# Two‑layer encoder in split float32: the token halves of the feed forward become the even and the odd tiles, block sums are made per pair of tiles, and the first products run in two column parts

## The chip, the cores and the metric

The kernel runs on one core of one Trainium2 chip. The metric is the device time of one execution in microseconds (us), as the median of several runs. Nothing else of the chip is used: no second core, no host arithmetic.

## What is computed

The reference is an encoder of two layers on 1024 tokens of width 1024 (float32). Each layer is

```
h = rmsnorm(x);  z = h @ w_in                       # 1024 -> Fourier 256, q 512, k 128, v 128, memory q 256
y = concat(fourier_mix, windowed attention (8 query heads, 2 kv heads, window 128, sink), attention to 256 memory rows)
x = x + rmsnorm(rmsnorm_per_group(y) @ w_out)
h = rmsnorm(x);  gate, up = split(h @ w_ffn_in)     # 1024 -> 2 x 2816
x = x + rmsnorm((silu(gate) * up) @ w_ffn_out)      # 2816 -> 1024
```

The order of the tokens matters in the mixing (window of 128, Fourier transform over the sequence). In the feed forward each token stands for itself.

## The kernel before

**Precision.** Every float32 operand is split in two (`split`, L149 to L152): ScalarE casts a high part (L151), VectorE or GpSimd subtracts it from the source and keeps the low part (L152). One product is three matmuls: high x high, high x low, low x high.

**Tiles.** The 1024 tokens are 8 tiles of 128. A tile's normalized rows are transposed on TensorE (L301 `hTp` in `norm_T` for the mixing, L1013 `hTp` in `Blocks.tile` for the feed forward).

**The feed forward's products** are made with seven block products in place of eight (a 2x2x2 scheme with sums). The activations are four blocks: `raw[half, kg]`, where `half` is a half of the tokens (four tiles, 512 columns) and `kg` a half of the 1024 channels. Before the change half 0 is tiles 0 to 3 and half 1 tiles 4 to 7. `Blocks.sum(i, c)` (L1016) makes the right operand of product i for column c, that is 128 of the 512 columns: products 2, 5, 7, 3 take a block as it is (and only split it), products 1, 4, 6 need a sum or difference first (L1031; `Blocks.last`, L1043 and L1044, then turns the raw blocks into what products 7 and 3 need). Products 2 and 4 need half 0 alone; 5, 1, 6, 7, 3 need half 1 too. The left operands are made by `Quad.weights` (a sum of two weight blocks on VectorE, L1074, then a split). One product is 12 matmuls of 512 columns (L1084). `Quad.step` puts the products together: PSUM tiles `qy` (products 2, 4), `qz` (5, 3), `qx` (1, 7), `qw` (6); `snap` copies one out (L1089). A layer has 11 pairs of quads, gate `gq` and up `uq`.

**From the attention to the feed forward.** The loop `for i in range(NT + 4)` in the main function does, for each i, one unit of the windowed attention (tile i), the output projection of tile i-2 (`mix.out`, PSUM `mo`, two residual and norm steps L988, L324, L325, L289), `hb.tile` of tile i-4, and from i = 8 on the block sums and the first products of the first pair: `gq.step(2)`, `gq.step(4)`, `uq.step(2)`, `uq.step(4)`.

**ffn_out** (L1212, PSUM `fo`) uses the same seven products over 22 x 128 channels; `abs_` is the ring of buffers for its split operands. The result of a tile is finished by `last_tile`: residual (L322 Square on ScalarE, L324 on VectorE, L325 add on GpSimd or VectorE), norm (L284, L289), store to `x2d`, and at the next tile the transposition `norm_T` into `nhT`. In the last product (i = 6) the four tiles of half 0 are finished one by one; those of half 1 follow after the last matmul. Between them stands `half()`, which is `mix.zf(0)` of the next layer: the first projection (PSUM `zT`, 48 matmuls of 512 columns) of tiles 0 to 3.

**What sets the order.** The program is one text; when it is built, a scheduler fixes the order of each engine's instructions, and the engines meet at semaphores. Memory is an arena of numbered places; `Ring(...)` lists the places that a kind of buffer goes through in turn, and a place that is still read holds up what is to be written there. DMAs start from the sync engine's (SP) queue in its order.

Of the kernel before, what the change touches and what calls it, by code (L numbers as in the profile page):

```python
# [39 lines left out]
SKEW = 1  # L40
N_SM = {"pos": 1}
# [27 lines left out]
def tile_encoder(ctx: ExitStack, tc: tile.TileContext, T, C, out):  # L69
# [60 lines left out]
    qws, sns, silus, acts = Ring(32, 0, 16, 20), Ring(36, 38, 40, 42, 32, 34), run(8, 5, 2), run(18, 7, 2)  # L130
    sums, wsums = run(8, 4, 2), Ring(4, 6)
# [4 lines left out]
    wcs, abs_ = Ring(112, 116, 96, 100, 48, 52, 56, 60), Ring(80)  # L136
# [170 lines left out]
    def residual_out(x, f, g, dst, t):  # L307
# [689 lines left out]
    class Blocks:  # L997


        HB = {2: (64, 72), 4: (80, 88), 5: (16, 24), 1: (0, 8), 6: (32, 40), 7: (None, None), 3: (None, 104)}  # L1000
# [4 lines left out]
        def tile(self, h, t):  # L1005
            half, c = divmod(t, 4)
# [9 lines left out]
        def sum(self, i, c, lo_eng=None):  # L1016
# [31 lines left out]
    class Quad:  # L1048


        def __init__(self, l, c0, hb):
            self.hb, self.c0 = hb, c0
# [38 lines left out]

        def step(self, i):

            if i == 2:
                self.y = ps([512], "qy", "pT")
                self.product(self.y, 2, True)
                self.s2 = self.snap(self.y)
            if i == 4:
                self.product(self.y, 4, False)
# [56 lines left out]
    def ffn_in(l, hb, actd, first):  # L1156

        for p in range(NFF // 2):
# [10 lines left out]
            if p == 0:  # L1169
                qws.ks, wsums.ks = (44, 48, 52, 56), (4, 6, 0, 2)  # L1170
# [263 lines left out]
```

## Time and profile before

| | |
|---|---|
| median of 3 runs | 2161.32 us (2158.72 to 2163.56) |
| profiled execution | 2151.62 us, of it 2149.5 us span from first to last instruction |
| mean granted TensorE clock | 0.969 of full |
| busy: TensorE / VectorE / ScalarE / GpSimd | 2007.0 / 1625.6 / 1070.4 / 846.9 us |
| chain that ended last | TensorE 73%, VectorE 8%, DMA 7%, GpSimd 4%, ScalarE 4%, issue 3% |

Busy time is what an engine's own instructions cover. PE is TensorE, PEld its weight loads, DVE VectorE, ACT ScalarE, POOL GpSimd, SP the sync engine. "Idle before" an instruction is the time in which its engine had nothing to run, and the name behind the arrow is what ended last before it started. The clock 1.00 is 2.4 GHz, 0.50 is 1.2 GHz; a stretch between them was partly at either.

### The profile page before, as it was taken

To read this page: it belongs to the slowest core of one execution; us is meant where nothing else is said; L and a number is where in the kernel's file an instruction comes from. 1 tells how busy PE (TensorE), PEld (TensorE's weight loads), DVE (VectorE), ACT (ScalarE), POOL (GpSimd) and SP (SyncE) were. 2 spreads that over 40 slices of the span, in tenths; PEclk is the share of its full clock that TensorE was granted. 3 is DMA by queue.
4 is the path that set the end of the run, shared out by engine and by line. 5 is a ranking of instruction groups with operands and counts; after the bars stand their busy time and mean duration, and the time that the engine had idled before them with its cause. 6 is when DMAs were issued, how large, how long until landed. Compare 5 with 4: busy or idle time off the path is not lost.

```text
span 2149.5 us, 28257 instructions
## 1 busy us (share of the span) xinstructions
PE 2007.0 (93%) x9402; PEld 1662.2 (77%) x9402; DVE 1625.6 (76%) x2517; ACT 1070.4 (50%) x2273; POOL 846.9 (39%) x854
## 2 busy tenths in 40 slices
PE   7998999699999999999989989986999999999997
PEld 6787787578888887878868768765888888878785
DVE  7569767998877877657866696779988787876774
ACT  6467767544333334444545686674433333345441
POOL 4244436633423334222454344464433343431322
PEclk9998999899999999999999999996999999999998
DMA  6111222412332326878641123133223232378874
GB/s 222 43 50 64 69 89 99 157 64 93 119 102 94 110 92 211 308 222 294 223 147 42 45 69 107 57 125 111 84 93 118 84 128 93 101 240 301 276 267 137
DMA packets 173602, 287.50 MB, mean 134 GB/s; under 512 B 15480, under 2 KB 73360, under 8 KB 173456
## 3 DMA queue, kind: packets, MB, share of 16 engines
q1 hardware_dynamic: 165392, 266.82, 37.7%
q10 hardware_dynamic: 8064, 18.88, 2.3%
q8 instruction: 74, 1.21, 0.2%
q14 instruction: 72, 0.59, 0.1%
HBM read 219.06 MB, written 66.58 MB: 133 GB/s over the span
## 4 chain that ended last, share of the span: by engine, by line
PE 73%; DVE 8%; DMA 7%; POOL 4%; ACT 4%; issue 3%; SPq 0%; POOLq 0%; ACTq 0%; DVEq 0%
PE fo L1212 12%; PE qz L1084 11%; PE qy L1084 11%; PE qx L1084 11%; PE mo L162 6%; PE qw L1084 5%; PE kvp L162 4%; PE qp L162 3%; DVE arena_r L152 3%; DMA arena_f<-actd 2%; PE sc L728 2%; PE av L772 2%; PE pT L765 1%; ACT arena_r L151 1%; DMA arena_f<-in_w_ffn_out 1%
## 5 line engine op out<-in xcount | busy, mean ns | idle before, releaser
L151 ACT CAST arena_r<-arena_f 128x512 fp32r<-128x512 f32 (+1 forms) x780 | 443.7, 591 | 689.6 <-PE qz L1084 117.2
L152 DVE TENSOR_TENSOR arena_r<-arena_f,arena_r 128x512 fp32r<-128x512 f32 (+1 forms) x676 | 539.4, 821 | 178.5 <-ACT arena_r L151 175.0
L1212 PE MATMUL fo<-arena_r 128*128 128x512 f32 x1848 | 430.9, 395 | 15.2 <-ACT arena_r L151 12.3
L1212 PEld LDWEIGHTS fo<-arena_r 128*128 128x128 f32 x1848 | 350.9, 191 | 91.7 <-ACT arena_r L151 14.8
L1084 PE MATMUL qy<-arena_r 128*128 128x512 f32 x1056 | 264.2, 399 | 24.3 <-ACT arena_r L151 16.5
L1084 PEld LDWEIGHTS qy<-arena_r 128*128 128x128 f32 x1056 | 202.8, 193 | 69.1 <-ACT arena_r L151 17.0
L1074 DVE TENSOR_TENSOR arena_f<-arena_f 128x512 f32<-128x512 f32 x220 | 210.0, 958 | 8.2 <-DMA arena_f<-in_w_ffn_in 3.2
L1084 PE MATMUL qz<-arena_r 128*128 128x512 f32 x704 | 196.2, 389 | 0.0
L1104 POOL TENSOR_TENSOR arena_f<-arena_f 128x512 f32<-128x512 f32 x44 | 70.1, 1593 | 305.8 <-ACT arena_f L1089 305.8
L1196 POOL TENSOR_TENSOR arena_f<-arena_f 128x512 f32<-128x512 f32 x50 | 74.0, 1481 | 267.2 <-DVE arena_r L152 134.7
L1084 PEld LDWEIGHTS qz<-arena_r 128*128 128x128 f32 x704 | 132.6, 188 | 27.6
L1136 POOL TENSOR_TENSOR arena_f<-arena_f 128x512 f32<-128x512 f32 x44 | 73.5, 1672 | 165.2 <-DVE arena_f L1116 127.3
L152 POOL TENSOR_TENSOR arena_r<-arena_f,arena_r 128x256 fp32r<-128x256 f32 (+2 forms) x104 | 85.5, 826 | 130.9 <-ACT arena_r L151 121.5
L1084 PE MATMUL qw<-arena_r 128*128 128x512 f32 x528 | 128.0, 390 | 3.0 <-ACT arena_r L151 3.0
L1084 PE MATMUL qx<-arena_r 128*128 128x512 f32 x528 | 127.3, 389 | 0.0
L1084 PE MATMUL qx<-big,arena_r 128*128 128x512 f32 x528 | 126.8, 389 | 0.0
L1084 PEld LDWEIGHTS qw<-arena_r 128*128 128x128 f32 x528 | 99.2, 188 | 23.9 <-ACT arena_r L151 3.2
L1084 PE MATMUL qz<-big,arena_r 128*128 128x512 f32 x352 | 115.7, 389 | 0.0
L1084 PEld LDWEIGHTS qx<-arena_r 128*128 128x128 f32 x528 | 99.1, 188 | 20.6
L1084 PEld LDWEIGHTS qx<-big,arena_r 128*128 128x128 f32 x528 | 99.1, 188 | 20.6
L162 PE MATMUL mo<-arena_r 128*128 128x512 f32 x384 | 104.8, 415 | 4.5 <-DVE arena_f L988 2.3
L162 PE MATMUL mo<-big,arena_r 128*128 128x512 f32 x384 | 102.7, 404 | 0.2 <-ACT arena_f L948 0.2
(218 smaller groups left out, 3592.8 us busy)
## 6 DMA issues: line engine op xcount, KB each, us to landing
arena_f<-in_w_ffn_out SPq DMA_DIRECT2D x264, 256.0 KB, 4.3
arena_f<-in_w_ffn_in SPq DMA_DIRECT2D x88, 512.0 KB, 3.6
actd<-arena_f SPq DMA_DIRECT2D x154, 256.0 KB, 3.8
arena_f<-actd SPq DMA_DIRECT2D x154, 256.0 KB, 4.2
arena_f<-in_w_in SPq DMA_DIRECT2D x40, 256.0 KB, 2.7
arena_f<-in_x SPq DMA_DIRECT2D x16, 512.0 KB, 4.0
arena_f<-in_w_out SPq DMA_DIRECT2D x32, 256.0 KB, 2.8
pmd<-arena_f ACTq DMA_DIRECT2D x32, 256.0 KB, 2.0
```

The lines of the kernel that those rows point to most:

```text
L151: nc.scalar.copy(hi, src)
L152: return (lo_eng or nc.vector).tensor_tensor(out=lo, in0=src, in1=f32(hi), op=ALU.subtract)
L162: mm(self.dst, a, b, start=self.i == 0, stop=self.i == self.n - 1)
L728: mm(pt, lhs, self.kst[g][i][:, k0 * P : k1 * P], start=i == 0, stop=i == 1)
L765: nc.tensor.transpose(pT[:, h, :], es_[h // 2][:, h % 2, j * P : j * P + P], ident)
L772: mm(av, lhs, p_, start=j == 0 and i == 0, stop=j == nk - 1 and i == 1)
L1074: nc.vector.tensor_tensor(out=s, in0=a, in1=b, op=op)
L1084: mm(pt, a, b, start=start and n == 0, stop=n == 11, skip_group_check=not start)
L1104: nc.gpsimd.tensor_tensor(out=self.v, in0=self.v, in1=self.s2, op=ALU.add)
L1136: (G if i in (0, 3) else V).tensor_tensor(out=a[i], in0=c, in1=g[i], op=ALU.mult)
L1196: (nc.vector, nc.gpsimd)[k % 2].tensor_tensor(out=s, in0=x, in1=y, op=op)
L1212: mm(pt, ab[:, 0, x, sl], ab[:, 1, y], start=new and first and j == 0, stop=last and j == 2, skip_group_check=not new)
```

## The change

1. `TILES = (0, 2, 4, 6, 1, 3, 5, 7)`: `Blocks.tile` puts tile t into half t mod 2, column t div 2. Half 0 is now the even tiles, half 1 the odd ones. `ffn_out` finishes the tiles in the order of `TILES`; n is the position in that order. `half()` (the next layer's `zf(0)`, still tiles 0 to 3) stands after the seventh tile in place of the sixth.
2. In the transition loop the sums for products 2 and 4 are made per pair of tiles as soon as an even tile is there (`i >= 4`), during the attention; those for 5, 1, 6 follow from i = 8 on, three columns ahead of the last tile, the fourth after the loop.
3. `product` takes a column slice, and weights are kept (`self.ws`). `ahead(i, sl)` runs product 2 or 4 of the first pair on columns 0 to 383 (three even tiles), and later on columns 384 to 511.
4. Places move: `HB` of products 4, 5 and 1, `qws` for the first weight loads (8, 12, 0, 44), `wcs` (88, 92 for 112, 116), `sums` (one place, then two, before four), `abs_` of ffn_out in layer 0 (nine places before six, and five for the last product) and in layer 1 (the same fifteen in another order).

```diff
@@ Blocks
-        HB = {2: (64, 72), 4: (80, 88), 5: (16, 24), 1: (0, 8), 6: (32, 40), 7: (None, None), 3: (None, 104)}
+        HB = {2: (64, 72), 4: (80, 112), 5: (0, 8), 1: (16, 24), 6: (32, 40), 7: (None, None), 3: (None, 104)}
...
-            half, c = divmod(t, 4)
+            c, half = divmod(t, 2)
@@ Quad
-        def product(self, pt, i, start):
-            w = self.weights(i)
+        def product(self, pt, i, start, sl=slice(0, 512)):
+            if i not in self.ws:
+                self.ws[i] = self.weights(i)
+            w = self.ws[i]
...
+        def ahead(self, i, sl):
+            if i == 2:
+                if sl.start == 0:
+                    self.y = ps([512], "qy", "pT")
+                    self.s2 = sns(512)
+                self.product(self.y, 2, True, sl)
+                nc.scalar.copy(self.s2[:, sl], self.y[:, sl])
+            else:
+                self.product(self.y, 4, False, sl)
@@ ffn_out
                 if i == 6 and k in (0, 2, 4, 6):
-                    t = (0, 2, 4, 6).index(k)
-                    out(t, fb[t][:, 0])
+                    out(k, fb[k // 2][:, 0])
...
         if not late:
-            out(4, fb[0][:, 1])
-            out(5, fb[1][:, 1])
+            out(1, fb[0][:, 1])
+            out(3, fb[1][:, 1])
+            out(5, fb[2][:, 1])
             half()
-            for p in range(2, 4):
-                out(4 + p, fb[p][:, 1])
+            out(7, fb[3][:, 1])
@@ the loop from the attention to the feed forward
+            c, odd = divmod(i - 4, 2)
+            if i >= 4 and not odd:
+                hb.sum(2, c)
+                hb.sum(4, c)
             if i == NT:
-                for c in range(4):
-                    hb.sum(2, c)
+                sums.ks = (40, 42)
+                gq.load()
+                gq.ahead(2, slice(0, 384))
+                for c in range(2):
+                    hb.sum(5, c)
             if i == NT + 1:
-                gq.load()
-                for c in range(4):
-                    hb.sum(4, c)
-                gq.step(2)
+                uq.load()
+                uq.ahead(2, slice(0, 384))
+                gq.ahead(4, slice(0, 384))
+                uq.ahead(4, slice(0, 384))
+                hb.sum(5, 2)
+                for c in range(3):
+                    hb.sum(1, c)
             if i == NT + 2:
-                uq.load()
-                gq.step(4)
-                uq.step(2)
-                uq.step(4)
-            if i >= NT:
-                for n in (5, 1):
-                    hb.sum(n, i - NT)
-            if i > NT:
-                for c in (i - NT - 1,) if i < NT + 3 else (2, 3):
+                for n in (2, 4):
+                    for q in first:
+                        q.ahead(n, slice(384, 512))
+                for c in range(3):
                     hb.sum(6, c)
                     hb.last(c)
+        for n in (5, 1, 6):
+            hb.sum(n, 3)
+        hb.last(3)
@@ ffn_out's ring, layer 1 then layer 0
-        abs_.ks = (64, 72, 80, 88, 16, 24, 0, 8, 32, 40, 48, 56, 96, 104, 112) if last else (80, 88, 48, 56, 96, 104)
+        abs_.ks = (64, 72, 80, 112, 0, 8, 16, 24, 88, 96, 32, 40, 48, 56, 104) if last else (64, 72, 80, 112, 88, 96, 48, 56, 104)
```

The order of instructions shows the moves best. In the rows below the first number is a line of the kernel's own text (after the change the lines of the helpers are two higher, and L1084 is L1082, L1013 is L1015, L1074 is L1070, L289 is L291).

TensorE in layer 0, from the last output projections (`mo` of tile 7 is the pair 4014/4028 before, 4039/4053 after) to the feed forward; `hTp` are the transpositions of the tiles, two per tile, the last two of tile 7. Before:

```order
L162 MATMUL mo_4028<-arena_r 128x512 x12
L1013 MATMUL hTp_4064<-const,arena_f 128x128 x4
L1084 MATMUL qy_4084<-arena_r 128x512 x2
L1013 MATMUL hTp_4111<-const,arena_f 128x128 x4
L1013 MATMUL hTp_4117<-const,arena_f 128x128 x4
L1084 MATMUL qy_4084<-arena_r 128x512 x22
L1084 MATMUL qy_4139<-arena_r 128x512 x2
L1013 MATMUL hTp_4180<-const,arena_f 128x128 x4
L1084 MATMUL qy_4139<-arena_r 128x512 x10
L1013 MATMUL hTp_4186<-const,arena_f 128x128 x4
L1084 MATMUL qw_4263<-arena_r 128x512
L1084 MATMUL qy_4139<-arena_r 128x512 x12
```

After:

```order
L164 MATMUL mo_4053<-arena_r 128x512 x8
L1082 MATMUL qy_4018<-arena_r 128x384 x2
L1015 MATMUL hTp_4083<-const,arena_f 128x128 x4
L1015 MATMUL hTp_4089<-const,arena_f 128x128 x4
L1082 MATMUL qy_4018<-arena_r 128x384 x10
L164 MATMUL mo_4053<-arena_r 128x512 x4
L1082 MATMUL qy_4018<-arena_r 128x384 x12
...
L1082 MATMUL qy_4097<-arena_r 128x128
L1015 MATMUL hTp_4235<-const,arena_f 128x128 x4
L1082 MATMUL qy_4018<-arena_r 128x128 x11
L1082 MATMUL qy_4097<-arena_r 128x128 x11
L1015 MATMUL hTp_4241<-const,arena_f 128x128 x4
```

The first products start before the last output projection is done, and all 48 + 48 of their matmuls stand ahead of the last transposition of tile 7; before, 12 of the 48 stood behind it.

VectorE in layer 0 at the first weight sum of the first pair (L1074 before, L1070 after; L988 and L990 finish `mo`, L289 and L291 are a tile's norm). Before:

```order
L988 SCALAR_TENSOR_TENSOR arena_f<-mo_4028,grs_3939,arena_f 128x512
L152 TENSOR_TENSOR arena_r<-arena_f,arena_r 128x4x128
L289 SCALAR_TENSOR_TENSOR arena_f<-arena_f,nrs_3982 128x1024
L1031 TENSOR_TENSOR arena_f<-big_3470,big_3992 128x512
L1044 TENSOR_TENSOR big_3985<-big_3985,big_3992 128x4x128
L152 TENSOR_TENSOR arena_r<-big_3992,arena_r 128x4x128
L1074 TENSOR_TENSOR arena_f<-arena_f 128x512
```

After:

```order
L990 SCALAR_TENSOR_TENSOR arena_f<-mo_3953,grs_3821,arena_f 128x512
L1070 TENSOR_TENSOR arena_f<-arena_f 128x512
L990 SCALAR_TENSOR_TENSOR arena_f<-mo_3967,grs_3821,arena_f 128x512
L154 TENSOR_TENSOR arena_r<-arena_f,arena_r 128x512
L1070 TENSOR_TENSOR arena_f<-arena_f 128x512
...
L990 SCALAR_TENSOR_TENSOR arena_f<-mo_4053,grs_3951,arena_f 128x512
```

The first weight sum moves from behind the last `mo` step to ahead of the last but one pair of them.

TensorE at the end of layer 0, from the last matmul of `fo` to `zT`, the next layer's first projection; `hTp` are the transpositions of the finished tiles (`big_6976` to `big_6979` before and `big_7026` to `big_7029` after hold four tiles at a time), `kvp` a tile's projection to keys and values (here tiles 0 and 1). Before:

```order
L1212 MATMUL fo_8517<-arena_r 128x512 x3
L301 MATMUL hTp_8685<-const,big_6977 128x128 x4
...
L301 MATMUL hTp_8871<-const,big_6979 128x128 x4
L301 MATMUL hTp_8878<-const,big_6979 128x128 x4
L162 MATMUL zT_8916<-arena_r 128x512
```

After:

```order
L303 MATMUL hTp_8928<-const,big_7029 128x128 x4
L303 MATMUL hTp_8952<-const,big_7026 128x128 x4
L303 MATMUL hTp_8959<-const,big_7026 128x128 x4
L303 MATMUL hTp_8983<-const,big_7027 128x128 x4
L164 MATMUL kvp_9248<-big_9214,arena_r 128x512
L164 MATMUL kvp_9285<-big_9214,arena_r 128x512
L303 MATMUL hTp_8990<-const,big_7027 128x128 x4
L164 MATMUL kvp_9248<-big_9214,arena_r 128x512 x3
L164 MATMUL kvp_9285<-big_9214,arena_r 128x512 x3
L164 MATMUL zT_8997<-arena_r 128x512
```

Before, `zT` follows the transpositions of four finished tiles; after, those of six (8952/8959 are the fifth, 8983/8990 the sixth), and eight matmuls of `kvp` move ahead of it.

## Rows read from the trace of the kernel before

**Rows 1.** The page: busy time of each engine, and the chain of waits that ended last.

```profile
PE 2007.0 (93%) x9402; PEld 1662.2 (77%) x9402; DVE 1625.6 (76%) x2517; ACT 1070.4 (50%) x2273; POOL 846.9 (39%) x854
PE 73%; DVE 8%; DMA 7%; POOL 4%; ACT 4%; issue 3%; SPq 0%; POOLq 0%; ACTq 0%; DVEq 0%
```

**Rows 2.** Stretches of the span: start and end, length, then busy us (and instructions) of PE, PEld, DVE, ACT, POOL, the granted clock, the DMA share and GB/s. 380 to 440 and 1450 to 1510 are the two transitions, 1085 to 1125 the change of layers, 845 to 860 the start of ffn_out in layer 0.

```profile
300.00:380.00 80.00, 73.14 (x393) 61.59 (x392) 60.53 (x136) 57.55 (x150) 49.24 (x70) 0.96 0.24 83
380.00:440.00 60.00, 37.52 (x160) 29.11 (x159) 54.84 (x69) 32.11 (x62) 32.92 (x29) 0.86 0.40 132
440.00:460.00 20.00, 20.00 (x90) 16.56 (x89) 18.98 (x28) 12.60 (x23) 4.29 (x3) 1.00 0.00 0
460.00:726.00 266.00, 266.00 (x1175) 220.28 (x1174) 213.83 (x255) 98.91 (x172) 99.27 (x64) 1.00 0.32 106
845.00:860.00 15.00, 11.53 (x39) 8.94 (x39) 13.06 (x14) 5.80 (x10) 11.37 (x8) 0.77 0.89 290
860.00:900.00 40.00, 39.53 (x192) 32.65 (x191) 30.79 (x42) 22.08 (x40) 12.70 (x11) 1.00 0.99 349
1125.00:1250.00 125.00, 119.83 (x617) 100.46 (x615) 84.19 (x153) 70.12 (x181) 53.29 (x71) 0.99 0.15 46
1250.00:1390.00 140.00, 127.03 (x664) 105.33 (x665) 104.97 (x285) 103.09 (x278) 57.95 (x98) 0.96 0.23 80
1390.00:1430.00 40.00, 36.13 (x195) 31.01 (x195) 31.81 (x68) 29.28 (x73) 22.34 (x33) 0.91 0.32 106
1430.00:1450.00 20.00, 15.64 (x90) 12.76 (x88) 14.11 (x24) 14.28 (x34) 17.93 (x22) 0.99 0.38 134
1450.00:1510.00 60.00, 42.84 (x154) 32.93 (x155) 55.18 (x71) 30.25 (x58) 27.14 (x24) 0.72 0.30 105
400.00:410.00 10.00, 4.61 (x25) 3.59 (x23) 6.78 (x8) 5.44 (x10) 6.87 (x8) 0.93 0.40 142
```

**Rows 3.** The time line of TensorE in layer 0's transition: start, length, engine and line, operation, output and inputs, count, and in brackets the idle time before it with what ended it.

```profile
414.67 1.22 PE L1084 MATMUL qy<-arena_r 128*128 128x512 f32 x2 [10.06 <-ACT arena_r L151]
423.72 3.47 PE L1084 MATMUL qy<-arena_r 128*128 128x512 f32 x14 [3.21 <-ACT arena_f L1089]
430.73 0.60 PE L1013 MATMUL hTp<-const,arena_f 128*128 128x128 f32 x4
434.33 0.50 PE L1084 MATMUL qw<-arena_r 128*128 128x512 f32 x1 [3.00 <-ACT arena_r L151]
434.82 4.62 PE L1084 MATMUL qy<-arena_r 128*128 128x512 f32 x12
```

**Rows 4.** VectorE's weight sums, line 1074, in layer 0 (380 to 440) and layer 1 (1440 to 1500): count, shortest, median and longest in ns, start of the first and of the last.

```profile
L1074 DVE TENSOR_TENSOR arena_f<-arena_f x11: 678/679/1757, 413.3 to 439.1; 128x512 f32<-128x512 f32 x11
L1074 DVE TENSOR_TENSOR arena_f<-arena_f x7: 678/693/2202, 1468.7 to 1498.5; 128x512 f32<-128x512 f32 x7
```

**Rows 5.** The time line of TensorE in layer 1's transition, columns as in rows 3.

```profile
1454.98 1.65 PE L772 MATMUL av<-arena_r 128*128 128x512 f32 x3 [5.82 <-DVE arena_r L152]
1491.14 1.22 PE L1084 MATMUL qy<-arena_r 128*128 128x512 f32 x2 [6.46 <-ACT arena_r L151]
1505.83 2.88 PE L1084 MATMUL qy<-arena_r 128*128 128x512 f32 x12
```

**Rows 6.** Groups of VectorE in layer 0's transition (376 to 440): count, busy us, mean ns, idle before.

```profile
L152 DVE TENSOR_TENSOR arena_r<-arena_f,arena_r 128x512 fp32r<-128x512 f32 x20 | 18.9, 986 | 1.2 <-ACT arena_r L151 1.2
L1044 DVE TENSOR_TENSOR big<-big,big 128x512 f32<-128x512 f32 x4 | 4.9, 1222 | 1.2 <-POOL arena_f L1031 1.2
L1031 DVE TENSOR_TENSOR arena_f<-big,big 128x512 f32<-128x512 f32 x7 | 4.7, 680 | 0.0
```

**Rows 7.** Time lines of VectorE and GpSimd around 1450, columns as in rows 3: the longest low part of that stretch and the GpSimd instruction that ran meanwhile; then a norm step with its next low part right behind it, and a run of two low parts.

```profile
1449.51 2.83 DVE L152 TENSOR_TENSOR arena_r<-big,arena_r 128x512 fp32r<-128x512 f32 x1
1449.07 2.72 POOL L325 TENSOR_TENSOR arena_f<-arena_f 128x1024 f32<-128x1024 f32 x1 [1.40 <-DVE arena_f L324]
1447.70 1.28 DVE L324 SCALAR_TENSOR_TENSOR arena_f<-arena_f,rrs 128x1024 f32<-128x1024 f32 x1 [0.72 <-POOL rrs L210]
1448.90 0.68 DVE L152 TENSOR_TENSOR arena_r<-arena_f,arena_r 128x512 fp32r<-128x512 f32 x1
1454.26 1.27 DVE L152 TENSOR_TENSOR arena_r<-pT,arena_r 128x512 fp32r<-128x512 f32 x2
```

**Rows 8.** Groups of TensorE from 300 to 440, both clocks mixed: count, busy us, mean ns of one (matmuls overlap, so a mean is longer than busy divided by count).

```profile
L1084 PE MATMUL qy<-arena_r 128*128 128x512 f32 x48 | 15.2, 470 | 13.9 <-ACT arena_r L151 10.1 <-ACT arena_f L1089 3.2 <-DVE arena_r L152 0.7
L1013 PE MATMUL hTp<-const,arena_f 128*128 128x128 f32 x64 | 11.8, 328 | 3.9 <-DVE arena_f L289 3.9
L728 PE MATMUL sc<-arena_r 128*128 128x384 f32 x38 | 10.4, 375 | 1.3 <-DVE rmax L729 1.3
L1084 PEld LDWEIGHTS qy<-arena_r 128*128 128x128 f32 x48 | 10.4, 226 | 17.3 <-ACT arena_r L151 10.3 <-ACT arena_f L1089 3.9 <-DVE arena_r L152 0.9
```

**Rows 9.** The time line of TensorE at the start of ffn_out in layer 0, columns as in rows 3.

```profile
847.09 2.88 PE L1212 MATMUL fo<-arena_r 128*128 128x512 f32 x12
853.44 6.79 PE L1212 MATMUL fo<-arena_r 128*128 128x512 f32 x17 [3.48 <-ACT arena_r L151]
```

**Rows 10.** The time lines of TensorE and, in the last three rows, VectorE and ScalarE from the last `fo` to `zT`, columns as in rows 3.

```profile
1088.82 1.97 PE L301 MATMUL hTp<-const,big 128*128 128x128 f32 x16 [2.87 <-DVE big L1243]
1095.64 9.20 PE L162 MATMUL zT<-arena_r 128*128 128x512 f32 x26 [4.85 <-ACT arena_r L151]
1104.67 1.04 PE L301 MATMUL hTp<-const,big 128*128 128x128 f32 x8
1112.42 1.90 PE L162 MATMUL kvp<-big,arena_r 128*128 128x512 f32 x7
1102.96 1.27 DVE L289 SCALAR_TENSOR_TENSOR big<-arena_f,nrs 128x1024 f32<-128x1024 f32 x1
1108.43 2.14 DVE L325 TENSOR_TENSOR arena_f<-arena_f,big 128x1024 f32<-128x1024 f32 x1 [4.20 <-DMA arena_f<-x1d]
1105.31 1.08 ACT L151 CAST arena_r<-hTp 128x512 fp32r<-128x512 f32 x2 [6.63 <-PE hTp L301]
```

More of the change, by code (lines that the diff above doesn't have):

```diff
@@ L40 @@
 SKEW = 1
+TILES = (0, 2, 4, 6, 1, 3, 5, 7)
 N_SM = {"pos": 1}
@@ L129, in tile_encoder @@
     sqs, pms, xfs = run(16, 2, 2), run(20, 2, 2), Ring(16, 20, 24, 28, 32, 0)
-    qws, sns, silus, acts = Ring(32, 0, 16, 20), Ring(36, 38, 40, 42, 32, 34), run(8, 5, 2), run(18, 7, 2)
-    sums, wsums = run(8, 4, 2), Ring(4, 6)
+    qws, sns, silus, acts = Ring(8, 12, 0, 44), Ring(36, 38, 40, 42, 32, 34), run(8, 5, 2), run(18, 7, 2)
+    sums, wsums = Ring(4), Ring(4, 6)
     ras, rbs, bsums, xs_ = run(40, 3, 2), run(46, 6, 2), Ring(58, 32, 34), Ring(36, 24)
@@ L311, in residual_out @@
         r = rsqrt_mean(ss, D, 1, "rrs")
-        for n in range(2):
-            ns = slice(n * 512, n * 512 + 512)
+        for i in range(2):
+            ns = slice(i * 512, i * 512 + 512)
             nc.vector.scalar_tensor_tensor(out=f[:, ns], in0=f[:, ns], scalar=r[:, 0:1], in1=g[:, ns], op0=ALU.mult, op1=ALU.mult)
-            (nc.gpsimd if t in (1, 3, 5) else nc.vector).tensor_tensor(out=x[:, ns], in0=x[:, ns], in1=f[:, ns], op=ALU.add)
-            (nc.sync, nc.scalar)[n].dma_start(dst[:, ns], x[:, ns])
+            (nc.gpsimd if n in (1, 3, 5) else nc.vector).tensor_tensor(out=x[:, ns], in0=x[:, ns], in1=f[:, ns], op=ALU.add)
+            (nc.sync, nc.scalar)[i].dma_start(dst[:, ns], x[:, ns])
     def residual(x, f, g, eng=None):
@@ L1082, in product @@
             for k in range(4):
-                for a, b in ((w[:, 0, k], bh[:, k]), (w[:, 0, k], bl[:, k]), (w[:, 1, k], bh[:, k])):
-                    mm(pt, a, b, start=start and n == 0, stop=n == 11, skip_group_check=not start)
+                for a, b in ((w[:, 0, k], bh[:, k, sl]), (w[:, 0, k], bl[:, k, sl]), (w[:, 1, k], bh[:, k, sl])):
+                    mm(pt[:, sl], a, b, start=start and n == 0, stop=n == 11, skip_group_check=not start)
                     n += 1
@@ L1090, in snap @@
             return s
-        def step(self, i):
[L1094 to L1099, printed above, removed]
+        def ahead(self, i, sl):
[5 more added lines that the diff above has]
+                nc.scalar.copy(self.s2[:, sl], self.y[:, sl])
+            else:
+                self.product(self.y, 4, False, sl)
+        def step(self, i):
+            if i in (2, 4):
+                self.ahead(i, slice(0, 512))
             if i == 5:
```

39 lines of the change are left out of this document (17 added, 22 removed).

## The prediction

> **What bounds the kernel now.** I read the busy shares first, then the stretches, then the time lines of the weak stretches. Over the span TensorE is busy 2007.0 of 2149.5 us and holds 73% of the chain of waits [rows 1], so only its 142 us of idle time and its slow clock can be won. The stretches show where these lie: the steady feed forward has none (266.00 of 266, clock 1.00), the two transitions from attention to feed forward lose most: 22.5 us of 60 at clock 0.86 in layer 0, 17.2 of 60 at 0.72 in layer 1 [rows 2]. In both VectorE is nearly full (54.84 and 55.18 of 60), and in layer 0 it stays so for the next 20 us (18.98) while TensorE is full as well. So a transition is bounded by VectorE: it has the last tiles' norms, the low parts and the first weight sums to do at once. TensorE's longest gaps wait for a cast that waits for a weight sum: 10.06 us in layer 0, 6.46 in layer 1 [rows 3, 5]; the first weight sums start only at 413.3 and 1468.7 [rows 4]. A mean of the whole span (VectorE 76%) does not show this.
>
> The sum is made against the profiled execution, 2151.62 us; the median of the runs, 2161.32, is 9.7 us above it, and I carry that over unchanged. A change of 0.2%, 4.3 us, is about what a measurement of this kernel can tell from none.
>
> **Layer 0's transition.** The first weight sum moves ahead of the last output projections, and all first products ahead of the last transposition of tile 7, behind which 12 of 48 stand now. Those 12 took 4.62 us and one `qw` 0.50 more, in the stretch 434.3 to 439.4 just before the last column is ready [rows 3]; taken away whole they are worth 5 us, the upper end. The lower end is zero: VectorE does the same work up to the last column's sums. Counting along its order from a common instruction of the attention, each with its distance to the next in an unbroken run (0.6 for low parts and sums of 0.68, 1.2 for norms of 1.28 [rows 7]), I get 60.2 us before and 60.7 after. Only VectorE's own idle time can then be won, and the nearest is 3.2 us of 400 to 410 [rows 2], just where the first weight sum, whose input is a load alone, now stands. I take 3, range 0 to 5. If TensorE gets no further ahead than VectorE makes weights, the gain is returned in 440 to 460; what is late next is the last column's split.
>
> **The matmuls cut in two.** 48 products of 512 columns become 48 of 384 and 48 of 128, per layer. By busy time per instruction, clocks mixed, 384 columns are 10.4/38 = 0.27 us, 128 columns 11.8/64 = 0.18 and 512 columns 15.2/48 = 0.32 [rows 8]: 48 x 0.13 = 6 us more of TensorE per layer; if columns alone counted it would be 0. All of it lies in the 22.5 and 17.2 us in which TensorE has nothing to do; I cost it at 0, up to 3 if that cover is gone in layer 1. A weight load takes 226 ns in this stretch [rows 8], longer than 128 columns of a matmul, so the load may set their pace: 48 x (0.27 + 0.23 - 0.32) = 8.6 us, which the cover still holds.
>
> **Layer 1's transition.** The same moves, but here VectorE has room before: it idles 8.2 us of 1390 to 1430 and 5.9 of 1430 to 1450 [rows 2]. Sums for three columns of products 2 and 4 go there: 9 instructions (two low parts and one difference each) at 0.68 [rows 4, 6] are 6.1 us. Along VectorE's order from the same tile's instruction the first weight sum comes 8.4 us of work earlier (50.8 to 42.4) and the last column 5.3 us earlier (73.7 to 68.4). Against this stand 17.2 us of idle and a clock of 0.72: twelve matmuls took 4.62 us in layer 0's transition and 2.88 at the end of this one [rows 3, 5]. The ends are 0 (the tile 7 chain of norm, transposition, copy and sums decides, not VectorE) and 14 (most of the idle and part of the clock). I take 7, between the two shifts of the order. What the moved instructions take there is open: alone a low part takes 0.68, but one took 2.83 while a GpSimd add of 2.72 ran [rows 4, 6, 7], and the mean of the differences on blocks is 1.22 [rows 6]. At 1.22 the nine are 11.0 us and still fit into the 14.1 of idle time of 1390 to 1450, so by the rows the term stays. The Trainium skill (SBUF — State Buffer, section Who interferes with whom) has it as a rule: a VectorE instruction with two SBUF inputs and a GpSimd instruction that reads SBUF shut each other out, and the later one waits for all of the other. The 2.83 beside 2.72 agrees. If that met all nine, they would take 25.5 us, 11.4 more than the room, and the sum would come out 11 higher; that is a rival below.
>
> **Start of ffn_out, layer 0.** Nine places for split operands in place of six let them be made earlier. TensorE waits 3.48 us at 850, and 29 matmuls take 9.67 us where 12 take 2.88 at full clock, so 2.7 us more are the clock's [rows 9]: at most 6.2. But DMA is at 0.89 there and at 0.99 in the next 40 us [rows 2], and more places bring no byte sooner once the queues are full. I take 2, range 0 to 6. In layer 1 the fifteen places are the same: 0. The store order and the tail after the last product keep their length: 0.
>
> **Change of layers.** This one costs. `zT` needs tiles 0 to 3. They were the first four finished; now tile 3 is the sixth. Before, TensorE waits 4.85 us and starts `zT` at 1095.64 [rows 10]. The sixth tile's norm ran at 1102.96 to 1104.23 [rows 10]; nothing ahead of it gets shorter, since its chain hangs on the last `fo`, which comes no earlier. Behind it stand two transpositions, a cast and a low part: 0.6 + 0.6 + 0.7, so `zT` starts at about 1106.1, 10.5 us later. Into that gap move 8 `kvp` (2.2 us by the row of seven in 1.90) and 1.0 us of transpositions that ran inside `zT` [rows 10], and 1.2 more of the sixth tile's own: 6.1 us of new idle remain. The residual add of the last tile waits for a load until 1108.43 and ends at 1110.5 [rows 10]; the second low part of tile 3 is queued behind it on VectorE, but `zT` can run its first 24 matmuls (5.4 us) without it. The ends: 10.5 if nothing fills in, 2 if the delay is taken up by the idle time of the next stretches (5.2 us in 1125 to 1250, 13.0 in 1250 to 1390 [rows 2]). I take 6.
>
> **Sum.** -3 - 7 - 2 + 6 = -6 us: 2145.6 of the profiled kind, 2155.3 as a median.
>
> **Rivals.**
> *The tile order decides.* Slower. The layer change costs its upper 10.5, and both transitions give together 0 to 4 because VectorE, nearly full until 460, takes the early matmuls' gain back: 10.5 - 2 - 0.5 = +8, 2169. It decides once `zT` starts later than about 1104 and the layer 1 transition gives under 4. For it speaks that TensorE is full from 1110 on before, so a delay has no slack near; against it, that 18 us of idle follow.
> *VectorE bounds all.* Same instructions, same end: the transitions give 0 to 2, ffn_out 1, the layer change takes 3 of its 6 from slack; +1, 2162. For it: 60.2 against 60.7 in the count of layer 0. Against: the count of layer 1.
> *Both transitions open up.* The long gaps of 10.06 and 6.46 close, the clock stays up, layer 1 gives 14 and layer 0 5, ffn_out 4, layer change +5: -18, 2143. For it: both gaps hang on the weight sum that moves. Against: VectorE's 5 us of idle per transition.
> *Low parts and sums meet GpSimd.* Slower. GpSimd is busier where the nine instructions go (17.93 of 20 in 1430 to 1450) than where they come from (27.14 of 60 [rows 2]). At 2.83 each [rows 7] they exceed the room of layer 1 by 11.4 us: -6 + 11 = +5, 2166. Against: it takes a GpSimd instruction beside every one, and GpSimd is idle for 17.7 of the 40 us of 1390 to 1430. The rule of the Trainium skill above (SBUF — State Buffer, section Who interferes with whom) is this case at its full size.
> *The change does not act.* The loads of the first weights may be held by places that are still read, or by a load of tile 7 ahead of them in SP's queue; then the first weight sum stays near 413 and the case is VectorE's, above.
>
> **How the numbers follow.** Forecast with its terms as sized: 0.40. VectorE bounds all, inaction included: 0.20. Both open up: 0.15. Tile order: 0.17. GpSimd: 0.08. Of the forecast's 0.40, 0.32 is below -4.3 us, since its terms spread by about 3 us around -6. Faster by over 0.2%: 0.32 + 0.15 = 0.47. Within: 0.08 + 0.16 = 0.24. Slower: 0.04 + 0.17 + 0.08 = 0.29. The forecast's own range is 2149 to 2161; the whole one, to leave out no more than 2 in 10, reaches into the open case and into the tile order, 2141 to 2168.
>
> **What would show it.** Right: first weight sum at 400 to 404 and about 8 us earlier relative to the attention in layer 1; the gap before the first `qy` under 5 us; `zT` starts 9 to 11 us after where it does now, relative to the last `fo`, with a gap of about 10 in TensorE. Wrong: the weight sum not earlier; VectorE's low parts over 1 us in the attention; `zT` late by under 5; a new gap at the first `qz` after tile 7 as long as the one removed.

## The result, and the profile after

The changed kernel takes 2168.97 us (median of 6 runs, 2165.29 to 2175.0) against 2160.4 us (6 runs, 2156.53 to 2163.56): ratio 1.0033, 95% interval 1.0017 to 1.0049, some 7 us slower by the ratio (8.6 between the medians). The forecast was 2155.3; the range ended at 2168.0. The profiled execution is 2167.86 us with a span of 2166.1. That of before (span 2149.5) lies under all its timed runs, so I compare with a second execution of the same program (b_copy below, span 2159.7) where a term is small.

The page of the changed kernel, busy time by engine [rows 1]:

```profile
PE 2025.7 (94%) x9498; PEld 1682.7 (78%) x9498; DVE 1623.9 (75%) x2517; ACT 1070.2 (49%) x2277; POOL 847.1 (39%) x854
```

TensorE is busy 18.7 us longer, for 96 more matmuls and at a mean clock of 0.960 in place of 0.969; VectorE does what it did. The stretches that answer to [rows 2], columns as there:

```profile
380.00:440.00 60.00, 45.94 (x218) 38.70 (x218) 53.25 (x66) 32.32 (x63) 33.99 (x30) 0.82 0.37 123
440.00:460.00 20.00, 19.79 (x75) 16.09 (x76) 18.55 (x26) 11.88 (x21) 5.45 (x4) 0.85 0.09 27
460.00:726.00 266.00, 266.00 (x1175) 220.26 (x1174) 214.41 (x258) 99.30 (x173) 98.41 (x64) 1.00 0.32 106
845.00:860.00 15.00, 8.67 (x39) 6.84 (x37) 13.66 (x21) 6.87 (x13) 3.30 (x3) 0.96 0.89 291
1100.00:1130.00 30.00, 19.13 (x88) 15.63 (x89) 21.35 (x23) 13.17 (x26) 19.66 (x17) 0.77 0.41 141
1460.00:1520.00 60.00, 45.19 (x211) 37.90 (x211) 55.00 (x69) 30.79 (x60) 25.75 (x24) 0.80 0.30 102
```

In layer 0's transition TensorE works 45.94 us in place of 37.52, but most of the difference is the cut: VectorE is as full as before. (The 48 `qy` of 15.2 us [rows 8] became two times 48 of 9.8 and 10.1 us, 4.7 of the 8.4 more.) The last row is layer 1's transition, where the program is 13.6 us later at its first `mo`. TensorE's time line in layer 0's transition [rows 3]:

```profile
410.18 0.51 PE L1082 MATMUL qy<-arena_r 128*128 128x384 f32 x2
414.88 2.38 PE L1082 MATMUL qy<-arena_r 128*128 128x384 f32 x12 [0.66 <-ACT arena_f L1097]
427.67 4.16 PE L1082 MATMUL qy<-arena_r 128*128 128x128 f32 x23 [1.74 <-DVE arena_r L154]
433.28 4.93 PE L1082 MATMUL qy<-arena_r 128*128 128x128 f32 x22
438.74 0.78 PE L1082 MATMUL qw<-arena_r 128*128 128x512 f32 x1
440.21 5.06 PE L1082 MATMUL qw<-arena_r 128*128 128x512 f32 x11 [0.69 <-DVE arena_r L154]
```

The gap of 10.06 us is gone, as said. The 128 column matmuls take 0.18 to 0.22 us each here, as the weight load's row had it: 0.22 (22 in 4.93) at 1.2 GHz (granted clock 0.50 from 433.2 to 438.2), while in layer 1 they take 0.12 (23 in 2.76 at 1505.91) at 2.4 GHz (1.00); in both stretches the weight loads fill the whole time. The next products start at 440 as before. At the start of ffn_out, at its last product, at the change of layers and in layer 1 [rows 9, 10, 5]:

```profile
850.79 2.88 PE L1217 MATMUL fo<-arena_r 128*128 128x512 f32 x12
860.76 9.40 PE L1217 MATMUL fo<-arena_r 128*128 128x512 f32 x30 [7.09 <-ACT arena_r L153]
...
1058.85 1.19 PE L1217 MATMUL fo<-arena_r 128*128 128x512 f32 x4 [1.63 <-ACT arena_r L153]
1061.38 18.58 PE L1217 MATMUL fo<-arena_r 128*128 128x512 f32 x69 [1.34 <-DVE arena_r L154]
...
1110.76 3.08 PE L303 MATMUL hTp<-const,big 128*128 128x128 f32 x12 [12.86 <-DVE big L291]
1116.72 6.52 PE L164 MATMUL zT<-arena_r 128*128 128x512 f32 x28
...
1478.48 2.07 PE L164 MATMUL mo<-arena_r 128*128 128x512 f32 x4 [7.75 <-ACT arena_r L153]
1505.91 2.76 PE L1082 MATMUL qy<-arena_r 128*128 128x128 f32 x23
```

The gap after the twelfth `fo` grew from 3.48 to 7.09; two gaps near 1060 are new; `zT` waits behind a gap of 12.86; and ahead of layer 1's `mo` stand 7.75 us, where before had 5.82 ahead of the `av` next to it [rows 5]. VectorE's weight sums [rows 4], columns as there:

```profile
L1070 DVE TENSOR_TENSOR arena_f<-arena_f x10: 677/680/1769, 404.9 to 441.3; 128x512 f32<-128x512 f32 x10
L1070 DVE TENSOR_TENSOR arena_f<-arena_f x11: 676/680/1761, 1479.3 to 1519.1; 128x512 f32<-128x512 f32 x11
```

**The span cut at matmuls.** One view settles most of what follows. Matmuls of a name are counted (`fo` 1 is the first of ffn_out, `fo` 924 the last of layer 0, `mo` 385 the first of layer 1, `qz` 1056 the last of the feed forward), and a row is the difference of two starts in one trace, in us:

```
                       before b_copy  after b_ring9 b_swap a_whole w_best d_contig
start to fo 1           847.1  850.4  850.8   851.3  852.4   848.9  850.9   852.7
fo 1 to 133              38.0   38.4   43.1    43.4   46.4    45.1   41.6    42.1
fo 133 to 749           157.1  157.2  152.8   153.9  157.2   155.0  155.1   156.9
fo 749 to 837            20.4   20.4   26.5    25.5   20.4    26.6   20.4    20.4
fo 837 to 924            22.0   22.9   22.1    21.1   22.1    21.1   22.6    22.7
fo 924 to mo 385        176.1  178.0  179.1   178.8  177.9   179.7  183.5   177.7
mo 385 to qz 1056       650.1  651.6  648.2   641.7  641.1   641.3  645.5   647.9
fo 925 to the end       238.4  240.5  243.2   240.5  241.7   243.3  235.4   239.8
span                   2149.5 2159.7 2166.1  2156.4 2159.5  2161.3 2155.2  2160.6
```

Two executions of before differ by 3.3 us up to `fo` 1 and by up to 2.1 in a later row. Against b_copy the change loses 5.6 us in layer 0's ffn_out (43.1 + 152.8 + 26.5 + 22.1 less 38.4 + 157.2 + 20.4 + 22.9), 1.1 to the first `mo`, 2.7 from `fo` 925 on, and wins 3.4 in layer 1.

### The profile page after: what moved, and what is told of

Read it like the earlier page. It is cut to its first block, busy times and chain, and to the rows that moved or that the text cites. A ratio compares the mean times of both kernels' runs of the same rounds, so it can differ in the third digit from the quotient of the medians.

```text
span 2166.1 us, 28419 instructions
## 1 busy us (share of the span) xinstructions
PE 2025.7 (94%) x9498; PEld 1682.7 (78%) x9498; DVE 1623.9 (75%) x2517; ACT 1070.2 (49%) x2277; POOL 847.1 (39%) x854
## 5 line engine op out<-in xcount | busy, mean ns | idle before, releaser
L1082 PE MATMUL qy<-arena_r 128*128 128x512 f32 (+2 forms) x1152 | 267.4, 382 | 9.1 <-DVE arena_r L154 4.2
L1082 PEld LDWEIGHTS qy<-arena_r 128*128 128x128 f32 x1152 | 213.4, 194 | 49.3 <-DVE arena_r L154 4.7
L1070 DVE TENSOR_TENSOR arena_f<-arena_f 128x512 f32<-128x512 f32 x220 | 210.9, 960 | 9.4 <-DMA arena_f<-in_w_ffn_in 2.4
L1082 PE MATMUL qz<-arena_r 128*128 128x512 f32 x704 | 196.2, 390 | 0.0
L1109 POOL TENSOR_TENSOR arena_f<-arena_f 128x512 f32<-128x512 f32 x44 | 65.8, 1496 | 305.4 <-ACT arena_f L1087 305.4
L1201 POOL TENSOR_TENSOR arena_f<-arena_f 128x512 f32<-128x512 f32 x50 | 72.0, 1440 | 268.1 <-DMA arena_f<-in_w_ffn_out 140.3
L1082 PEld LDWEIGHTS qz<-arena_r 128*128 128x128 f32 x704 | 132.3, 188 | 27.6 <-ACT arena_r L153 0.2
L1141 POOL TENSOR_TENSOR arena_f<-arena_f 128x512 f32<-128x512 f32 x44 | 73.0, 1659 | 169.3 <-DVE arena_f L1121 132.0
L1082 PE MATMUL qw<-arena_r 128*128 128x512 f32 x528 | 133.1, 401 | 3.1 <-DVE arena_r L154 1.2
L1082 PE MATMUL qx<-arena_r 128*128 128x512 f32 x528 | 127.6, 389 | 0.0
L1082 PE MATMUL qx<-big,arena_r 128*128 128x512 f32 x528 | 126.8, 389 | 0.0
L1082 PEld LDWEIGHTS qw<-arena_r 128*128 128x128 f32 x528 | 102.4, 194 | 26.5 <-DVE arena_r L154 2.4
L1082 PE MATMUL qz<-big,arena_r 128*128 128x512 f32 x352 | 115.6, 389 | 0.0
L1082 PEld LDWEIGHTS qx<-big,arena_r 128*128 128x128 f32 x528 | 99.1, 188 | 20.6
L1082 PEld LDWEIGHTS qx<-arena_r 128*128 128x128 f32 x528 | 99.1, 188 | 20.6
```

Source lines behind the costliest of these rows:

```text
L1070: nc.vector.tensor_tensor(out=s, in0=a, in1=b, op=op)
L1082: mm(pt[:, sl], a, b, start=start and n == 0, stop=n == 11, skip_group_check=not start)
L1109: nc.gpsimd.tensor_tensor(out=self.v, in0=self.v, in1=self.s2, op=ALU.add)
L1141: (G if i in (0, 3) else V).tensor_tensor(out=a[i], in0=c, in1=g[i], op=ALU.mult)
L1201: (nc.vector, nc.gpsimd)[k % 2].tensor_tensor(out=s, in0=x, in1=y, op=op)
```

## The experiments

**b_copy**, the kernel before once more. 

> The kernel before, once more, to see how far two executions of one program differ stretch by stretch. The profiled execution of before (2151.62 us) lies below all its timed runs; if that is chance, this one is nearer to 2160, and the stretches that then differ by more than 2 us cannot be read from one pair of traces. Ratio to before 1.000 within 0.001.

 Measured: ratio 1.0004 (0.9993 to 1.0015), span 2159.7. The first profiled execution of before was shorter by 3.3 us up to `fo` 1 and by 0.8 to 2.1 in four later rows.

**b_ring9**, before with the ring of the change alone:

```diff
-... else (80, 88, 48, 56, 96, 104)
+... else (64, 72, 80, 88, 112, 96, 48, 56, 104)
...
             if i == 7:
+                abs_.i, abs_.ks = 0, (80, 88, 96, 104, 112)
```

> The kernel before with the ring of nine places and the five for the last product, and nothing else changed. Theory ring and queue: ffn_out of layer 0 alone makes most of the loss: fo 1 to 924 takes 243 to 246 us in place of 239, with the slow pieces at fo 749 to 837 and a gap of about 7 us after the twelfth fo; ratio 1.002 to 1.003. Rival tile order and transitions: fo 1 to 924 at 239 or less, ratio 0.999 to 1.001.

 Measured: 0.9994 (0.9984 to 1.0004). Both theories are half right. ffn_out of layer 0 loses as foretold (43.4, 25.5, in all 243.9 in place of 239.0), with no tile order and no cut. The piece `fo` 749 to 837 belongs to the ring; the start, `fo` 1 to 133, need not, since b_swap below has 46.4 there with the six places of before. But layer 1's attention and feed forward, in which nothing was edited, are 9.9 us shorter, so the whole shows nothing.

**a_ring7, a_place6**: the changed kernel with 64 and 72 left out of the ring; for a_ring7

```diff
-(64, 72, 80, 112, 88, 96, 48, 56, 104)
+(80, 112, 88, 96, 48, 56, 104)
```

and for a_place6

```diff
-(64, 72, 80, 112, 88, 96, 48, 56, 104)
+(80, 112, 48, 56, 96, 104)
```

> The changed kernel without places 64 and 72 in layer 0's ffn_out ring (seven places, the five of the last product as in the change). The next layer's first weights (w_in, places 64 to 80) can then be loaded at the start of ffn_out again. Theory queue: in the changed kernel the load of w_in waits in SP's queue at 1053 for the ring to leave 64 and 72, the loads of actd behind it come late, and fo 749 to 837 take 26.5 us in place of 20.4. Then these two pieces take 20.4 here, and fo 1 to 924 about 238 to 240 us in place of 244.5; time 2161 to 2165, ratio 1.000 to 1.002. Rival (the five places of the last product cause it, or DMA bounds the whole): the pieces stay at 26 and the ratio at 1.003.

 

> The changed kernel with six places in layer 0's ffn_out ring, (80, 112, 48, 56, 96, 104), and the five of the last product as in the change. 80 and 112 are free early, as the first two places of before; 88 and 92 hold the last weights of the last quad in the changed kernel and are left out, as 112 and 116, the last ones of before, are there; 64 and 72 are left to the next layer's first weights. Theory places: fo 1 to 133 falls from 43.1 to 38 to 40 us, fo 749 to 837 from 26.5 to 20 to 22, fo 353 to 749 rises to 94.6; ratio 0.999 to 1.001. Rival (the ring of five in the last product, or the tile order, costs by itself): fo 749 to 924 stays at 48 us and the ratio at 1.002 or more.

 Measured: 1.0086 (1.007 to 1.0102) and 1.004 (1.0026 to 1.0055). `fo` 749 to 837 is 21.8 and 20.4: places 64 and 72 in the ring cost that piece. In the change, the SP queue around 1050 (start, length, line, transfer), then ScalarE:

```profile
1046.76 1.89 SPq L1189 DMA_DIRECT2D arena_f<-in_w_ffn_out  x4
1053.27 0.38 SPq L341 DMA_DIRECT2D arena_f<-in_w_in  x1
1054.51 3.91 SPq L353 DMA_DIRECT2D arena_f<-in_w_in  x3
1059.02 0.33 SPq L1183 DMA_DIRECT2D arena_f<-actd  x1
```

```profile
1051.25 1.14 ACT L153 CAST arena_r<-arena_f 128x512 fp32r<-128x512 f32 x2 [6.25 <-PE fo L1217]
1053.97 0.62 ACT L153 CAST arena_r<-arena_f 128x512 fp32r<-128x512 f32 x1 [1.58 <-PE fo L1217]
1056.10 0.62 ACT L153 CAST arena_r<-arena_f 128x512 fp32r<-128x512 f32 x1 [1.50 <-DMA arena_f<-in_w_in]
1057.67 1.12 ACT L153 CAST arena_r<-arena_f 128x512 fp32r<-128x512 f32 x2
```

The next layer's first weights (w_in) are split into places 64 to 79. With 64 and 72 in the ring that split waits until `fo` has read them for the last time. ScalarE stands 6.25 us for that, casts the four pieces of w_in (the first four casts; their low parts are made on GpSimd), and only then, at 1057.67, two operands of the last product, whose loads went out by 1048.7 and had landed by 1052.3. These casts end TensorE's gap of 1.63. The SP queue stands too, from 1048.7 to 1053.3, before the fourth load of w_in, which waits 4.6 us for one of those low parts on GpSimd, and the load of `actd` behind it goes out at 1059.0. That is after the first gap had ended, and the second one (1.34) ends with a low part of what was cast by 1058.8: in the trace the casts hold TensorE up, not the queue. With the slow clock it is 6.1 us in all.

Both runs are slower as a whole, though, and a_ring7 missed what was expected of it (20.4, 238 to 240 and 2161 to 2165): its ffn_out takes 256.7. `fo` 1 to 133 is 52.1, and 45.3 in a_place6 (38 to 40 expected). And what a_ring7 wins at `fo` 749 to 837 it loses at once: `fo` 837 to 924 takes 28.6 in place of 22.1, with a gap of 5.48 at 1085.0 behind a late load of `actd`, after the SP queue had stood from 1069.9 to 1075.3 before the store of a finished tile. With six places that piece is short as well (23.1 in a_place6).

**a_nine88**: the nine places with 88 last, `(64, 72, 80, 112, 48, 56, 96, 104, 88)`. 

> The changed kernel with the same nine places in layer 0, but 88 last: (64, 72, 80, 112, 48, 56, 96, 104, 88). Theory: place 88, which holds the last weights of the feed forward, stands fifth in the change and holds up the casts behind it. Then fo 1 to 133 falls from 43.1 to 40 or less here; fo 749 to 837 stays at 26. Rival (nine places load too far ahead and crowd the transfers): fo 1 to 133 stays at 43. Ratio 1.001 or 1.003.

 Measured: 1.0061 (1.0049 to 1.0073), `fo` 1 to 133 49.1. My theory that place 88 holds up the start falls. `fo` 749 to 837 is 22.8, where 26 was expected.

**a_ring6**: six places of before in the changed kernel. 

> The changed kernel with the six places (80, 88, 48, 56, 96, 104) for split operands in layer 0's ffn_out that before had, and no new ring for its last product. Theory ring: the gap of 7.1 us after the twelfth fo falls to about 3.5 and the stretch from the first to the last fo from 244.5 to about 238, time 2162 to 2166, ratio about 1.001. Rival (the stretch is bounded by DMA and its length is chance, or set by the order of the loads): stretch and time as in the changed kernel, ratio 1.003.

 Measured: 1.0093 (1.0072 to 1.0113). Here 48 and 56 are also written by the next layer's transposed tiles, which now come there during the last product, so part of both is overwritten and the end of the product waits (`fo` 837 to 924 36.5); nothing is concluded from it.

**a_by_n**: `norm_T` takes the index n in place of `TILES[n]`, and `half()` stands one tile earlier. 

> The changed kernel, but the next layer takes the tiles in the order in which they are finished, and zf(0) stands after the sixth tile again, as before the change (the attention of layer 1 then sees the tiles in another order: the output is that of permuted tokens). Theory tile order decides: zT starts about 11 us after the last fo, as before, not 21, and the time falls by 3 to 10 us against the changed kernel, 2159 to 2166, ratio to before 0.999 to 1.002. Rival (the delay is taken up by later idle time, and the loss comes from ffn_out and the transitions): zT starts early but the time stays at 2167 to 2171, ratio 1.003.

 Measured: 1.0049 (1.0035 to 1.0063). `zT` starts early (from the last `fo` to the 32nd `zT` 19.8 us, 28.7 in the change), yet `fo` 924 to `mo` 385 is only 2.9 shorter and layer 1's attention takes 213.8 from its first to its last `mo`, 3.9 longer.

**a_ring1**: layer 1's places in the order of before. 

> The changed kernel with layer 1's fifteen places for split operands in the order of before. Theory: the order of the places sets when the first loads can start, and ffn_out of layer 1 (fo 925 to 1848) falls from 226.8 to about 224; ratio to before 1.002. Rival (chance, or DMA): 226 to 228, ratio 1.003.

 Measured: 1.0021 (1.0012 to 1.003), `fo` 925 to 1848 221.2 in place of 226.8. The stretch bears the theory out, and so do the other traces, with ranges that just touch: 225.1 to 228.5 in the nine kernels with the change's order of the fifteen places, 220.6 to 225.7 in the others. That it is by the loads is not shown. Of the whole some 3 us are left, with intervals that touch.

**a_whole**: the first products uncut, on 512 columns after the last even tile. 

> The changed kernel with the first products uncut: each runs on all 512 columns after the last even tile. It has 96 matmuls less. If the cut is what gains in layer 1's transition, the stretch from the first mo of layer 1 to its last qz grows from 648 to 651 or more, and the ratio is 1.004 to 1.006. If the cut gains nothing (VectorE bounds the transition): the stretch stays within 1 us, ratio 1.003.

 Measured: 1.0018 (1.0007 to 1.0028), about 3 us under the change, with intervals that touch. The cut wins nothing that shows; layer 1's 641.3 probably came with another order there, as in b_ring9 and b_swap.

**c_contig**: halves of consecutive tiles in the changed kernel, with its places and rings. 

> The changed kernel's places and rings, but halves of tiles 0 to 3 and 4 to 7 as before; sums for products 2 and 4 right after each of tiles 0 to 3, during the attention, and the first products uncut, from i = 8 on. The tile order's wait for zT is gone and VectorE still has the sums out of the transition. If the early sums help and only the tile order harms: ratio to before 0.994 to 0.998. If VectorE bounds the transitions whatever the order: 1.000. If the new rings harm: 1.002 or more, with ffn_out of layer 0 longer by 5 us than before.

 Measured: 1.004 (1.0025 to 1.0054), with `fo` 1 to 924 at 245.4. As in b_ring9 that is shown for `fo` 749 to 837 (25.3): there the new ring harms without the tile order too.

**w_place6, w_best, d_contig**: a_whole with the six places; that with layer 1's order `(64, 72, 80, 112, 16, 24, 0, 8, 32, 40, 48, 56, 96, 104, 88)`; and that with contiguous halves, which also brings back before's loop of the later sums and `half()` after the sixth tile:

```diff
-TILES = (0, 2, 4, 6, 1, 3, 5, 7)
+TILES = tuple(range(8))
...
-            c, half = divmod(t, 2)
+            half, c = divmod(t, 4)
...
+            if 4 <= i < NT:
+                hb.sum(2, i - 4)
+                hb.sum(4, i - 4)
...
```

> a_whole (first products uncut) with the six places of a_place6. If the gain of layer 1 in a_whole (641 us from its first mo to its last qz, 651.5 before) and that of the six places add up: 2150 to 2155, ratio 0.995 to 0.998, faster than both kernels. If a change in layer 0's ring orders layer 1 anew and its gain goes: that stretch returns to 648 to 651 and the ratio to 1.000.

 

> w_place6 with layer 1's fifteen places ordered with 88 last: (64, 72, 80, 112, 16, 24, 0, 8, 32, 40, 48, 56, 96, 104, 88). Theory places: fo 925 to 1101 falls from 49.7 in a_whole to 44 to 46, and the whole lies 3 to 5 us below w_place6. Rival (DMA bounds ffn_out of layer 1, what is gained at its start is lost at fo 1277 to 1365): within 2 us of w_place6.

 

> w_best (uncut first products, six places in layer 0's ffn_out, layer 1's places ordered anew) with halves of tiles 0 to 3 and 4 to 7 in place of even and odd ones; the sums for products 2 and 4 follow tiles 0 to 3 during the attention. If the tile order costs what the layer change shows, the stretch from layer 0's last fo to layer 1's first mo falls from 183.5 to about 178 and the time by 3 to 6 us: ratio to before 0.997 to 0.999. If that delay is taken up later, or the even and odd halves gain as much in the transitions: 1.000.

 Measured: 1.0017 (1.0009 to 1.0026), 1.0002 (0.9993 to 1.001), 0.9991 (0.9981 to 1.0002). The gains did not add up in w_place6 (2150 to 2155 expected; its layer 1 stretch is 646.4). w_best lies 3.0 us below it, as expected, with `fo` 925 to 1101 at 45.5. w_best and d_contig differ in the tile order and in what hangs on it: `fo` 924 to `mo` 385 is 183.5 against 177.7. I take that as the cost of the tile order, 5.8 us. In the other traces the row goes the same way, with ranges that just touch: 176.1 to 179.7 in the seven with halves of consecutive tiles, 179.1 to 184.9 in the nine with even and odd ones (a_by_n, with its own order, has 176.2). The tile order gives back 3.4 us from layer 1's last `mo` to the last `qz` (436.1 against 439.5), and the whole differs by about 2 us, with intervals that touch.

**b_swap**: before with two places exchanged, `(80, 88, 48, 56, 104, 96)`. 

> The kernel before with the last two of layer 0's six ffn_out places exchanged (104 before 96). The amount of work is the same everywhere; built anew, some 660 of layer 1's matmuls from the attention to the feed forward stand in another order. If the order that the scheduler happens to give decides layer 1's attention: its stretch from the first mo to the last qz moves by 3 us or more off 651.5, with the ratio between 0.995 and 1.005. If the order there hardly matters and the edits made the differences: 650 to 653, ratio 0.999 to 1.001.

 Measured: 0.9994 (0.9985 to 1.0003). With the same work and sizes, `mo` 385 to `qz` 1056 falls by 10.5 and `fo` 1 to 133 rises by 8.0. TensorE's waits at the start of ffn_out:

```profile
863.92 18.52 PE L1212 MATMUL fo<-arena_r 128*128 128x512 f32 x72 [8.60 <-ACT arena_r L151]
885.30 9.95 PE L1212 MATMUL fo<-arena_r 128*128 128x512 f32 x36 [2.85 <-ACT arena_r L151]
```

The gaps are of the size of the change's (7.09), in the program of before. So at these two places the order that the scheduler gives outweighs what was edited. The 38 us of `fo` 1 to 133 stand in the two executions of before alone; the other fifteen kernels, whatever their edit, take 40.9 to 52.1.

**t_swap2**: the exchange only after the first product. 

> The kernel before with the same two ring places exchanged, but only after the first product of layer 0's ffn_out. The order of layer 1's attention is then that of b_swap in its middle part (324 matmuls moved), while most of the first product's order is that of before. If the two effects are separate: fo 1 to 133 about 38 to 41 us, the first mo to the last qz of layer 1 about 641 to 645, and the whole 2150 to 2155, ratio 0.995 to 0.998. If they belong together: 46 and 641, or 38 and 651, ratio 0.999 to 1.001.

 Measured: 0.9988 (0.9974 to 1.0001): 40.9 and 642.7. Most of both can be had at once, but `fo` 133 to 749 is 4 longer and the whole is not clear of no change. No version beat the kernel before clearly; the best ones lie at 0.999.

## Why the prediction was wrong

Against b_copy the change's span is 6.4 us longer, where 6 less were forecast. Of these 12.4 us, 7.6 lie in layer 0's ffn_out, 7.0 in the two transitions and 2.7 in layer 1's ffn_out; the change of layers came out 4.9 cheaper than sized.

*Start of ffn_out, "I take 2, range 0 to 6": this step failed.* Measured against b_copy, layer 0's ffn_out lost 5.6, and the range had no loss in it. The new list of places moved the split of the next layer's weights (w_in), with the last of its loads, from the start of ffn_out to its last product, ahead of casts that TensorE needs next: +6.1 at `fo` 749 to 837. Seven kernels with 64 and 72 among nine places take 22.8 to 26.7 there, nine without them 20.4 to 21.8, and in six of the seven ScalarE stands 6.2 to 6.5 us before the first cast of w_in (in a_nine88, with 22.8, the order is another). That w_in is split into 64 to 79 could be read in the program; the sum did not count it. The start, +4.6, is within what order alone does, as b_swap shows; what in the order makes it stays open (number of places and place 88 were tried and do not explain it). The nine places did win 4.4 in between (`fo` 133 to 749: 152.8 to 155.0 in the seven, 155.1 to 161.3 with six).

*Layer 0's transition, 3, and layer 1's, 7: these failed too; neither gained.* Counted from the 241st and the 625th `mo`, the first of tile 5 in each layer, to the first `fo` of ffn_out, layer 0 takes 519.3 and 519.5 us in the two executions of before and 520.1 in the change, layer 1 519.2 and 520.1 against 520.1. In layer 0 the first weight sum came to 404.9, one us past the foretold window (74.2 us after `mo` 241 in place of 85.5), and the gap of 10.06 closed. But the last low part of a block came 114.1 us after it in place of 111.9, and the products after tile 7 still start at 440. "VectorE bounds all" was right here.

In layer 1 the term counted nine instructions as moved from the transition into the attention. The text of the program has them there only after the change, but the scheduler had put them there before. These are VectorE's first low parts of blocks, before and after:

```profile
1404.31 0.69 DVE L152 TENSOR_TENSOR arena_r<-big,arena_r 128x512 fp32r<-128x512 f32 x1
1416.03 0.69 DVE L152 TENSOR_TENSOR arena_r<-big,arena_r 128x512 fp32r<-128x512 f32 x1
1425.46 0.69 DVE L152 TENSOR_TENSOR arena_r<-big,arena_r 128x512 fp32r<-128x512 f32 x1 [1.11 <-ACT arena_r L151]
```

```profile
1417.09 0.69 DVE L154 TENSOR_TENSOR arena_r<-big,arena_r 128x512 fp32r<-128x512 f32 x1
1427.45 0.68 DVE L154 TENSOR_TENSOR arena_r<-big,arena_r 128x512 fp32r<-128x512 f32 x1
1442.10 2.80 DVE L154 TENSOR_TENSOR arena_r<-big,arena_r 128x512 fp32r<-128x512 f32 x1
```

From `mo` 625 (1391.9 and 1402.8) they stand at 12.4, 24.1 and 33.5 us before and at 14.3, 24.7 and 39.3 after; the first weight sum is at 76.7 and 76.5, not 8 us earlier, and the last low part of a block at 109.0 and 112.7. This is shown for three of the nine. The 3.4 us of the row `mo` 385 to `qz` 1056 are won further ahead, between the 577th and the 625th `mo` (31.3 in b_copy, 27.8 in the change), and are not shown to come from the sums, since an exchange of two ring places gives 10.5 in that row.

*The cut, 0:* right. Its price per instruction was as worked out (0.18 to 0.22 us), and the cover hid it: from the 337th `mo`, the first of tile 7, to `fo` 1 it is 466.5 us in both executions of before, 466.3 in the change and 465.3 in a_whole, which has no cut.

*Change of layers, 6.* `zT` starts 21.4 us after the last `fo` in place of 11.0, 10.4 later, where 10.5 was worked out (8.9 later than in b_copy, 12.5), and with the rings matched the net cost is 5.8. In the change itself only 1.1 is left; the trace does not say why. The rival "tile order decides" named 2169 us, which is what was measured, but by luck: its reason, a layer change at its full 10.5, is not what made the time.

*ffn_out of layer 1, 0: measured 2.7*; "the fifteen places are the same" overlooked that their order counts (a_ring1).

*GpSimd's lock (the Trainium skill, SBUF — State Buffer, section Who interferes with whom)*: VectorE's busy time is 1623.9 in place of 1625.6, so no loss of that kind shows. One of the low parts above ran long beside a GpSimd add (2.80 at 1442.10, the add 2.77), as one did before (2.83 [rows 7]).

## What to carry to other kernels

When a list of places or a loop is edited, read the whole order of every engine and queue before and after, and price each cast and transfer that moves, also those of other layers: one that waits for a place holds up all that stands behind it, as the casts of w_in did on ScalarE. Before a gain is counted from instructions that move, look in the trace of before whether they are still where the program's text has them. Cut the span at the same matmuls in both traces, since stretches of time mix effects of both signs; and before a few us are put down to an edit, measure an edit that changes nothing but the order.

## What was not expected of the hardware

TensorE's clock stood at 0.77 from 1100 to 1130, where it had waited 12.86 us before, and at 0.89 from 1040 to 1070 in the changed kernel against 1.00 in before over the same 30 us of the span, beside gaps of only 1.63 and 1.34 us:

```profile
1040.00:1070.00 30.00, 27.02 (x109) 21.76 (x108) 18.70 (x22) 14.84 (x30) 18.96 (x15) 0.89 0.59 188
```

So of the 6.1 us lost in `fo` 749 to 837 3.0 were those gaps; the slower clock goes with the rest (0.11 of 30 us is 3.3 us at full clock).
